# Row of `c` in the weights' queue, modulation products three loads behind and fewer at first, four places for the squares: one change in five parts to a diffusion layer on one core

## The chip, the core and the metric

The kernel runs on one core of one Trainium2 chip. The metric is the device time of one execution in microseconds (us). The engines are called PE (TensorE), DVE (VectorE), ACT (ScalarE), POOL (GpSimd) and SP (SyncE, which here only issues transfers). Each works through its own instructions in order and waits at semaphores for the others.

## What is computed

One layer for 1024 tokens of width 1024, with 256 context tokens. The parts of the reference that matter here:

```python
mod = jax.nn.silu(c) @ w_mod[l] + b_mod[l]                  # 6 x 1024 values from one row
mod_c = jax.nn.silu(c_ctx) @ w_mod[l, :, :2 * D_MODEL] + b_mod[l, :2 * D_MODEL]
h = x * (1.0 + scale1) + shift1
proj = h @ w_in + b_in                                      # q_a, k_a, v_a, q_b, k_b, v_b, gates
q_b = _rope_2d(_qk_rms(heads(OFF_QB, OFF_KB, B_HEADS), q_norm_g), rope)

def _qk_rms(t, g):
    tf = t.astype(jnp.float32)
    return (tf * lax.rsqrt(jnp.mean(tf * tf, axis=-1, keepdims=True) + QK_EPS) * g).astype(t.dtype)
```

Then follow windowed attention (A), global attention (B), their gated merge, a LayerNorm and a gated feed-forward part with a convolution. The change doesn't touch these.

## The kernel before

**Numbers in two parts.** Each matrix is split into a high part (a rounded copy, made by ACT, names `wh...`, `hh...`) and a low part (the rest, names `wl...`, `hl...`, made by DVE, for the gates by POOL). Each product takes three matmuls of 128x512: high by high, high by low, low by high (L90 to L92 in `mm3`). `split` (L82 to L87) makes the parts.

**Modulation.** The 48 columns of the modulation are no matmuls but *products* on DVE: `mod` (L188) multiplies a 128x1024 tile of weights (512 KB, by a DMA of SP) by the row `sc` (Silu of `c`, spread over the partitions by `spread`) or `scc` (the same of `c_ctx`) and sums along it. A second small instruction reads the sum out. The first 16 columns are needed for `h` and are made in the first stage, two per k. The other 48 products (16 of them with `scc` for the context, in `modx`; 32 in `modc`) are *late*: tiles `wml...`, numbered downwards from 47.

**First stage, `q1acc`.** It makes the queries of B. `load1(k)` issues, on SP's queue, two weight tiles of the modulation (`wm`), the weights `wr` and the tile `xr` of x; `modulate(k)` splits the weights, makes two products and from them `hh` and `hl` (ACT L217, L218; DVE L219). For each of eight k, 24 matmuls go into eight accumulators `q1acc0` to `q1acc7`. The row of `c` is loaded through ACT's queue (L179).

**After it.** `q_evac` moves the accumulators to `Q` with a bias (DVE L301). The PE then works through an order of gates (`g`, a column block of the gates, 48 matmuls) and products with further weights: three gates, then `qa` (queries of A, eight k of four token tiles, accumulators `accqa`), four gates, `qb` (the same for the other four token tiles, `accqb`), four gates, then `ka`, a gate, `kb` and four gates. `prefetch` loads and splits the weights of what comes later; `wg` and `wqa` share three places.

**Beside this,** the queries of B are finished in steps that `side_step` hands out. `rms_scale` makes the squares of a tile (ACT L282, into `sqq`), sums them over a head (DVE L285), divides by 64 and adds eps (DVE L286) and raises to the power -0.5 (POOL L287); then the signs are turned (POOL L322). `rope` turns a tile (L263, twice L269, L271), on POOL for tiles 2 and 5, else on DVE, with tables `tbq` that POOL makes (L274, L279). There is one tile `sqq` with places for two token tiles, so that the squares of the next wait for the sums of the one before.

**Late products.** After every gate half and every k, `mods(us)` adds that piece's matmuls to a running sum `span[0]`, and issues as many late products, load and multiplication together, as belong to its share of the whole (`span[1]`, which ends with `ka`). The places of these tiles are shared with the gates' results `sg`.

The program's order in each engine is made by a scheduler out of these pieces, so that the order in the code is not always the order on the chip.

Of the kernel before, what the change touches and what calls it, by code (L numbers as in the profile page):

```python
# [9 lines left out]
AF = mybir.ActivationFunctionType  # L10
ALU = mybir.AluOpType
# [51 lines left out]
VOFF = 0.0  # L63
VSPAN = 1.0
VSC = 0, 1
DNS = {u0 + 2 * n + (u0 == 20): (n, j0, j1) for u0, j0, j1 in ((16, 0, 4), (20, 4, 8), (24, 8, 11)) for n in range(3)}


@with_exitstack
def layer_kernel(  # L70
# [66 lines left out]
    def hput(*names):  # L137
        for n in names:
            hfree.append(hslot.pop(n))
# [21 lines left out]
    def wsplit(wr, nm, le="vector"):  # L161
        wh = ph1.tile([P, 512], R32, tag="wp", name=f"wh{nm}", bufs=8)
        wl = ph1.tile([P, 512], R32, tag="wp", name=f"wl{nm}", bufs=8)
        split(wr, wh, wl, nc.scalar, getattr(nc, le))
        return wh, wl
# [10 lines left out]
    def spread(dst, src, n):  # L176
        row = ht(f"row{n}")
        hput(f"row{n}")
        nc.scalar.dma_start(row, src.partition_broadcast(P))  # L179
        nc.scalar.activation(dst, row, AF.Silu)  # L180

    def tmp(name):
# [4 lines left out]
    def mod(w, row, bias, o):  # L187
        nc.vector.tensor_tensor_reduce(out=w, in0=w, in1=row, scale=1.0, scalar=bias, op0=ALU.mult, op1=ALU.add,  # L188
                                       accum_out=o)
# [5 lines left out]
    def load1(k):  # L195
        wm = []
        for j in (0, 1):
            w = tmp(f"wm{j}_{k}")
            nc.sync.dma_start(w, wmodT[j * 8 + k])
            wm.append(w)  # L200
        x = tmp(f"xr{k}")
        wr = raw(f"wr{k}")
        nc.sync.dma_start(wr, w_qb[k])
        nc.sync.dma_start(x, xT[k])
        st1[k] = wm, x, wr

    def modulate(k):
        wm, x, wr = st1.pop(k)
        w = wsplit(wr, f"qb{k}")
        for j in (0, 1):  # L210
            col = j * 8 + k
            mod(wm[j], sc, bmc[:, col:col + 1], modc[:, col:col + 1])
        hh = hTp.tile([P, T], R32, tag="hT", name=f"hh{k}", bufs=16)
        hl = hTp.tile([P, T], R32, tag="hT", name=f"hl{k}", bufs=16)
        a, b = modc[:, k:k + 1], modc[:, 8 + k:9 + k]
        for s in [slice(0, HALF), slice(HALF, T)] if k == 0 else [slice(0, T)]:
            nc.scalar.activation(hh[:, s], x[:, s], AF.Identity, bias=a, scale=b)  # L217
            nc.scalar.activation(x[:, s], x[:, s], AF.Identity, bias=a, scale=b)  # L218
            nc.vector.tensor_tensor(out=hl[:, s], in0=x[:, s], in1=hh[:, s].bitcast(F32), op=ALU.subtract)  # L219
        hT.append((hh, hl))  # L220
        return w
# [57 lines left out]
            eng.tensor_tensor(out=dv[:, :, a, :], in0=sv[:, :, a, :], in1=gv[:, :, 1 - a, :], op=ALU.mult)  # L279

    def rms_scale(x3, H, nm, sq, ss=None):
        nc.scalar.activation(sq.rearrange("p (h d) -> p h d", d=HD), x3, AF.Square)  # L282
        if ss is None:
            ss = ph1.tile([P, 8], F32, tag="ss", name=f"ss{nm}", bufs=4)[:, 0:H]
        nc.vector.tensor_reduce(out=ss, in_=sq.rearrange("p (h d) -> p h d", d=HD), axis=AX.X, op=ALU.add)  # L285
        nc.vector.tensor_scalar(out=ss, in0=ss, scalar1=1.0 / HD, scalar2=QK_EPS, op0=ALU.mult, op1=ALU.add)  # L286
        nc.gpsimd.tensor_tensor(out=ss, in0=ss, in1=mhalf[:, 0:H], op=ALU.pow)  # L287
        return ss

# [16 lines left out]
    def qpost(br, t):  # L306
        q = qtile(br, t)
        q3 = q.rearrange("p (h d) -> p h d", d=HD)
        if br == 0:
            def r0():  # L310
                rope(nc.gpsimd if t % 3 == 2 else nc.vector, q, q, 8, ropec[:, t], ropes[:, t], f"q0_{t}")
            return [r0]
        st = {}

        def s1():
            st["tb"] = ph1.tile([P, 2, HD], F32, tag="tb", name=f"tbq{t}", bufs=4)
            gfold(st["tb"], 0, t, nc.gpsimd)
            rms_scale(q3, 8, f"q{t}", sqq[0][:, t % 2], pqs[:, t])
            if t == NT - 1:
                sqq.clear()  # L320
                hput("sqq")
            nc.gpsimd.tensor_scalar(out=nqs[:, t], in0=pqs[:, t], scalar1=-1.0, scalar2=0.0, op0=ALU.mult, op1=ALU.add)  # L322

        def s2():
            tb = st["tb"]
            rope(nc.gpsimd if t % 3 == 2 else nc.vector, q, q, 8, tb[:, 0], tb[:, 1], f"q1_{t}")
        return [s1] + [lambda: None] * GAP + [s2]

    sqq = [ht("sqq", (P, 2, 512))]
    bias_qb = bias_tile(b_qb, "bias_qb")  # L330
    for t in range(NT):
        q_evac(1, t, acc[t], bias_qb)
# [308 lines left out]
    total = len(late)  # L641
    span = [0.0, 0.0]

    def mods(us):
        span[0] += us
        n = total - len(late)
        for _ in range(min(int(total * span[0] / span[1] + 0.01) - n, len(late))):
            col, row, o = late.pop(0)
            w = tmp(f"wml{len(late)}")
            nc.sync.dma_start(w, wmodT[col])  # L650
            mod(w, row, bmc[:, col:col + 1], o)
            if not late:
                hput("sc", "scc")
                kv_alloc()

# [1059 lines left out]
```

## Time and profile before

| what | us |
|---|---|
| three runs | 1610.99, 1612.0, 1614.45 |
| median | 1612.0 |
| the profiled execution | 1612.16 |
| its span in the trace | 1610.4 |
| granted clock of PE, mean over the span | 0.988 |
| first matmul begins | 12.94 |
| eight evacuations of `q1acc` (L301) | 54.23 to 59.68 |
| mean of a late product beside other work, 59.6 to 101.2 | 1.422 |

The prediction shows the rows of the profile. In lists of waits a row names the engine and line that waited, what it waited for, and then the sum in us, the times, and the longest wait. In the chain a row is start, length, engine, tile and line. In the timeline a row is start, length, engine, line, operation, out<-in, with the idle time ahead of it and its cause in brackets. In groups, after the bar, stand the busy time in us and the mean in ns of one instruction. Line numbers are those of the kernel before; in the change they are 2 higher from L66 on (the product L188 is L190, a split's L87 is L89) and 6 higher in the functions of the queries (L285 is L291, L286 is L292, L287 is L293, L269 is L275, L271 is L277).

### The profile page before, as it was taken

Reading aid. Unit: us, or ns where it says so; the run is one execution under the profiler, and the core shown is the slowest. Engines: PE = TensorE matmul, PEld = TensorE weight load, DVE = VectorE, ACT = ScalarE, POOL = GpSimd, SP = SyncE. Lnnn points to the kernel's source line nnn. Section 1 sums busy time; section 2 is a strip of 40 time slices with the busy share of each in tenths; the row PEclk is TensorE's granted clock in tenths of the full one; section 3 lists DMA queues with packets and bytes.
Section 4 is the critical chain, followed back from the end, with each engine's and each line's share of the span. In section 5 each row is a group of like instructions: output and inputs, shape, how many; then the busy total and the mean of one; then the engine's idle time right before and its main releaser. Section 6 shows DMA issues by size and latency. Waiting matters only on the chain.

```text
span 1610.4 us, 22060 instructions
## 1 busy us (share of the span) xinstructions
PE 1536.3 (95%) x7680; PEld 1275.4 (79%) x7680; DVE 1197.2 (74%) x1766; ACT 814.6 (51%) x1443; POOL 745.3 (46%) x731
## 2 busy tenths in 40 slices
PE   6999999999999999999999989899999999999996
PEld 5878788888877787777788877688888888888886
DVE  7797646538888777888675787588888888657886
ACT  5422222458887667688322464344544444435542
POOL 0573302526666556655323464366667765021141
PEclk9999999999999999999999999999999999999998
DMA  9695662322237555430560212233334446996821
GB/s 377 214 311 190 214 211 82 121 76 64 62 108 171 126 135 132 114 79 19 174 196 7 87 65 105 92 106 105 105 105 105 106 117 175 370 272 204 260 99 53
DMA packets 112367, 229.98 MB, mean 143 GB/s; under 512 B 12960, under 2 KB 27808, under 8 KB 112160
## 3 DMA queue, kind: packets, MB, share of 16 engines
q1 hardware_dynamic: 96816, 198.93, 37.0%
q0 software_dynamic: 10400, 20.19, 8.1%
q10 hardware_dynamic: 5040, 9.46, 1.6%
q8 instruction: 60, 0.98, 0.3%
q14 instruction: 51, 0.42, 0.1%
HBM read 177.35 MB, written 65.86 MB: 151 GB/s over the span
## 4 chain that ended last, share of the span: by engine, by line
PE 73%; DVE 10%; ACT 4%; issue 4%; DMA 4%; POOL 3%; SPq 0%; ACTq 0%; DVEq 0%; POOLq 0%
PE ptr L531 4%; PE p L92 4%; PE p L91 4%; PE p L90 4%; PE b L92 3%; PE b L91 3%; PE b L90 3%; PE g L90 2%; PE g L91 2%; PE g L92 2%; PE c L90 2%; PE c L92 2%; PE c L91 2%; PE d L90 2%; PE d L92 2%
## 5 line engine op out<-in xcount | busy, mean ns | idle before, releaser
L541 DVE TENSOR_TENSOR ptl<-ptr,pth 128x512 fp32r<-128x512 f32 x188 | 124.8, 686 | 27.7 <-ACT pth L540 25.4
L531 PE MATMUL ptr<-ident,p 128*128 128x128 f32 x816 | 126.8, 278 | 9.4 <-DVE ptl L541 6.9
L540 ACT CAST pth<-ptr 128x512 fp32r<-128x512 f32 x188 | 106.6, 588 | 56.4 <-PE ptr L531 32.8
L87 DVE TENSOR_TENSOR ld<-rd,hd 128x1024 fp32r<-128x1024 f32 x77 | 94.1, 1241 | 52.6 <-ACT hd L82 50.4
L426 ACT ACTIVATE p<-p,nm 128x1024 f32<-128x1024 f32 (+2 forms) x128 | 125.5, 982 | 11.1 <-DVE p L459 10.4
L531 PEld LDWEIGHTS ptr<-ident,p 128*128 128x128 f32 x816 | 93.7, 140 | 39.9 <-DVE ptl L541 14.0
L82 ACT CAST hd<-rd 128x1024 fp32r<-128x1024 f32 x77 | 79.4, 1053 | 81.2 <-PE p L92 51.3
L552 PE MATMUL av<-pth,VT 128*128 128x512 f32 x236 | 104.6, 443 | 1.1 <-ACT avs L558 0.5
L90 PE MATMUL p<-hd 128*128 128x512 f32 x264 | 103.2, 391 | 0.0
L92 PE MATMUL p<-hd,ld 128*128 128x512 f32 x264 | 102.7, 389 | 0.0
L91 PE MATMUL p<-ld,hd 128*128 128x512 f32 x264 | 102.7, 389 | 0.0
L90 PE MATMUL g<-hh,whg 128*128 128x512 f32 x256 | 99.9, 390 | 0.0
L92 PE MATMUL g<-hh,wlg 128*128 128x512 f32 x256 | 99.7, 389 | 0.0
L91 PE MATMUL g<-hl,whg 128*128 128x512 f32 x256 | 99.6, 389 | 0.0
L553 PE MATMUL av<-ptl,VT 128*128 128x512 f32 x236 | 97.7, 414 | 2.0 <-POOL ptl L87 1.9
L87 POOL TENSOR_TENSOR wlg<-wg,whg 128x512 fp32r<-128x512 f32 x32 | 44.4, 1393 | 111.8 <-ACT whg L82 111.8
L459 DVE TENSOR_SCALAR_CACHE_REDUCE p<-s,cvt,nmc 128x1024 f32<-128x1024 f32 x64 | 84.5, 1340 | 12.3 <-PE s L415 11.8
L414 PE MATMUL s<-KL,q 128*128 128x512 f32 (+2 forms) x192 | 76.0, 396 | 2.9 <-ACT p_x L426 2.0
L188 DVE CUSTOM_DVE_ANT_0 wml<-wml,sc,bmc 128x1024 f32<-128x1024 f32 x32 | 44.0, 1387 | 39.3 <-DMA wml<-in_wmodT_dram 38.8
L84 POOL TENSOR_SCALAR pth<-prw 128x512 fp32r<-128x512 f32 x48 | 31.2, 650 | 87.8 <-ACT prw L537 62.2
L82 ACT CAST wA<-ru 128x512 fp32r<-128x512 f32 x57 | 35.6, 625 | 71.4 <-PE d L92 33.7
L415 PE MATMUL s<-KL,q 128*128 128x512 f32 (+2 forms) x192 | 71.7, 373 | 0.0
(396 smaller groups left out, 4997.2 us busy)
## 6 DMA issues: line engine op xcount, KB each, us to landing
wml<-in_wmodT_dram SPq DMA_DIRECT2D x48, 512.0 KB
ru<-in_w_up_dram SPq DMA_DIRECT2D x38, 512.0 KB
rd<-td SPq DMA_DIRECT2D x55, 256.0 KB
rd<-sd SPq DMA_DIRECT2D x44, 256.0 KB
rd<-in_w_dn_dram SPq DMA_DIRECT2D x33, 256.0 KB
wm<-in_wmodT_dram SPq DMA_DIRECT2D x16, 512.0 KB
wg<-in_w_g_dram SPq DMA_DIRECT2D x32, 256.0 KB
sgd<-sg ACTq DMA_DIRECT2D x32, 256.0 KB
```

The costliest lines, as they stand in the source:

```text
L82: nc.scalar.copy(hi, src)
L87: lo_eng.tensor_tensor(out=lo, in0=src, in1=hi.bitcast(F32), op=ALU.subtract)
L90: nc.tensor.matmul(ps, a[0], b[0], start=start, stop=False, skip_group_check=resumed)
L91: nc.tensor.matmul(ps, a[0], b[1], start=False, stop=False, skip_group_check=resumed)
L92: nc.tensor.matmul(ps, a[1], b[0], start=False, stop=stop, skip_group_check=resumed)
L426: nc.scalar.activation(p, s, AF.Exp, bias=nm[:, h:h + 1], scale=scale, accum_out=sm[:, h:h + 1])
L459: nc.vector.tensor_scalar(out=p, in0=o, scalar1=self.qscale(nqs)[:, hs] if self.br else -1.0, scalar2=self.other[:, hs], op0=ALU.mult, op1 ...
L531: nc.tensor.transpose(tr[:, h * P:(h + 1) * P], self.pslice(h, n), ident)
L540: nc.scalar.copy(hi, tr)
L541: nc.vector.tensor_tensor(out=lo, in0=tr, in1=hi.bitcast(F32), op=ALU.subtract)
L552: nc.tensor.matmul(self.av, v, hi, start=first, stop=False)
L553: nc.tensor.matmul(self.av, v, lo, start=False, stop=self.left == 0)
```

## The change

Five parts:

1. `spread` loads the rows through SP's queue instead of ACT's: the row of `c` becomes SP's first transfer; that of `c_ctx` comes behind the loads of k = 4.
2. For k = 0, x is loaded in two halves, and the split of the weights stands behind the two products.
3. In `rms_scale`, the division by 64 moves into the Square's scale, and the addition of eps moves from DVE to POOL (18 instructions).
4. Two tiles `sqq0`, `sqq1` with two places each, instead of one.
5. `mods` issues the late loads by the share to the power 1.4 (`MODP`), so fewer early and more late, and each product is issued three loads behind its load (`MODL`), the rest at the end.

```diff
+MODP = 1.4
+MODL = 3
...
     def spread(dst, src, n):
         row = ht(f"row{n}")
         hput(f"row{n}")
-        nc.scalar.dma_start(row, src.partition_broadcast(P))
+        nc.sync.dma_start(row, src.partition_broadcast(P))
         nc.scalar.activation(dst, row, AF.Silu)
...
         nc.sync.dma_start(wr, w_qb[k])
-        nc.sync.dma_start(x, xT[k])
+        for s in [slice(0, HALF), slice(HALF, T)] if k == 0 else [slice(0, T)]:
+            nc.sync.dma_start(x[:, s], xT[k][:, s])
...
         wm, x, wr = st1.pop(k)
-        w = wsplit(wr, f"qb{k}")
+        if k:
+            w = wsplit(wr, f"qb{k}")
         for j in (0, 1):
             col = j * 8 + k
             mod(wm[j], sc, bmc[:, col:col + 1], modc[:, col:col + 1])
+        if not k:
+            w = wsplit(wr, f"qb{k}")
...
-        nc.scalar.activation(sq.rearrange("p (h d) -> p h d", d=HD), x3, AF.Square)
+        nc.scalar.activation(sq.rearrange("p (h d) -> p h d", d=HD), x3, AF.Square, scale=HD ** -0.5)
...
-        nc.vector.tensor_scalar(out=ss, in0=ss, scalar1=1.0 / HD, scalar2=QK_EPS, op0=ALU.mult, op1=ALU.add)
+        nc.gpsimd.tensor_scalar(out=ss, in0=ss, scalar1=1.0, scalar2=QK_EPS, op0=ALU.mult, op1=ALU.add)
...
-            rms_scale(q3, 8, f"q{t}", sqq[0][:, t % 2], pqs[:, t])
+            rms_scale(q3, 8, f"q{t}", sqq[t // 2 % 2][:, t % 2], pqs[:, t])
...
-    sqq = [ht("sqq", (P, 2, 512))]
+    sqq = [ht(f"sqq{n}", (P, 2, 512)) for n in (0, 1)]
...
+    wmq = []
+
     def mods(us):
         span[0] += us
         n = total - len(late)
-        for _ in range(min(int(total * span[0] / span[1] + 0.01) - n, len(late))):
+        for _ in range(min(int(total * min(span[0] / span[1], 1.0) ** MODP + 0.01) - n, len(late))):
             col, row, o = late.pop(0)
             w = tmp(f"wml{len(late)}")
             nc.sync.dma_start(w, wmodT[col])
-            mod(w, row, bmc[:, col:col + 1], o)
-            if not late:
+            wmq.append((w, row, bmc[:, col:col + 1], o))
+        while len(wmq) > (MODL if late else 0):
+            mod(*wmq.pop(0))
+            if not late and not wmq:
                 hput("sc", "scc")
                 kv_alloc()
```

The scheduler puts much else in another order with it. Three places matter for what follows. First PE, at the last k of the first stage, where an accumulator's last matmul is the one with `hl7`. Before:

```order
L90 MATMUL q1acc0_173<-whqb7_448,hh7_454 128x512
L91 MATMUL q1acc0_173<-wlqb7_449,hh7_454 128x512
L92 MATMUL q1acc0_173<-whqb7_448,hl7_455 128x512
L90 MATMUL q1acc1_174<-whqb7_448,hh7_454 128x512
L91 MATMUL q1acc1_174<-wlqb7_449,hh7_454 128x512
L92 MATMUL q1acc1_174<-whqb7_448,hl7_455 128x512
```

In the change, the same place from the ninth of its 24 matmuls on:

```order
L92 MATMUL q1acc4_178<-whqb7_449,hh7_455 128x512
L93 MATMUL q1acc4_178<-wlqb7_450,hh7_455 128x512
L92 MATMUL q1acc5_179<-whqb7_449,hh7_455 128x512
L94 MATMUL q1acc0_174<-whqb7_449,hl7_456 128x512
L94 MATMUL q1acc1_175<-whqb7_449,hl7_456 128x512
L94 MATMUL q1acc2_176<-whqb7_449,hl7_456 128x512
```

The matmuls with `hl7` moved behind the others of five tiles: `q1acc0` is complete at the 12th matmul of the 24 instead of the 3rd, `q1acc1` at the 13th instead of the 6th.

Second DVE, around the low part of the weights of `qa` for k = 2 (`wlqa2`). Before:

```order
L263 TENSOR_TENSOR rt1q1_4_975<-Q1_4_531,tbq4_930 128x512
L269 TENSOR_TENSOR rt2q1_4_976<-Q1_4_531,tbq4_930 128x16x16 x2
L285 TENSOR_REDUCE cvt_70<-sqq_522 128x8
L271 TENSOR_TENSOR Q1_4_531<-rt1q1_4_975,rt2q1_4_976 128x512
L286 TENSOR_SCALAR cvt_70<-cvt_70 128x8
L188 ISA wml33_1078,modx_63<-wml33_1078,scc_144,bmc_61 128x1024
L188 ISA modx_63 128x1
L87 TENSOR_TENSOR wlqa2_824<-wqa2_821,whqa2_823 128x512
```

In the change:

```order
L269 TENSOR_TENSOR rt1q1_6_1154<-Q1_6_536,tbq6_1068 128x512
L275 TENSOR_TENSOR rt2q1_6_1155<-Q1_6_536,tbq6_1068 128x16x16 x2
L291 TENSOR_REDUCE cvt_70<-sqq1_524 128x8
L277 TENSOR_TENSOR Q1_6_536<-rt1q1_6_1154,rt2q1_6_1155 128x512
L190 ISA wml38_1105,modx_63<-wml38_1105,scc_144,bmc_61 128x1024
L190 ISA modx_63 128x1
L190 ISA wml37_1148,modx_63<-wml37_1148,scc_144,bmc_61 128x1024
L190 ISA modx_63 128x1
L89 TENSOR_TENSOR wlqa2_811<-wqa2_808,whqa2_810 128x512
```

`wlqa2` stood behind the rope of tile 4 (and 13 late products in all); now it stands behind the rope of tile 6 (and 11 products). The first `rt2q1_6` waits on a semaphore for POOL's last step of the rope of tile 5.

Third POOL, from the second tile's power on (L287 before, L293 in the change). Before:

```order
L287 TENSOR_TENSOR cvt_70<-cvt_70,mhalf_73 128x8
L322 TENSOR_SCALAR cvt_70<-cvt_70 128x8
L87 TENSOR_TENSOR wlg2_0_640<-wg2_0_637,whg2_0_639 128x512
L263 TENSOR_TENSOR rt1q1_2_870<-Q1_2_528,tbq2_812 128x512
L87 TENSOR_TENSOR wlg2_1_646<-wg2_1_643,whg2_1_645 128x512
```

In the change:

```order
L89 TENSOR_TENSOR wlg1_1_565<-wg1_1_562,whg1_1_564 128x512
L292 TENSOR_SCALAR cvt_70<-cvt_70 128x8
L293 TENSOR_TENSOR cvt_70<-cvt_70,mhalf_73 128x8
L328 TENSOR_SCALAR cvt_70<-cvt_70 128x8
L269 TENSOR_TENSOR rt1q1_2_857<-Q1_2_530,tbq2_799 128x512
L275 TENSOR_TENSOR rt2q1_2_858<-Q1_2_530,tbq2_799 128x16x16 x2
```

`wlg1_1` moved from ahead of the first power to ahead of the second, each power has its addition of eps (L292) ahead of it on POOL, and the rope of tile 2 moved ahead of the splits `wlg2_0` and `wlg2_1`.

More of the change, by code (lines that the diff above doesn't have):

```diff
@@ L317, in s1 @@
             gfold(st["tb"], 0, t, nc.gpsimd)
-            rms_scale(q3, 8, f"q{t}", sqq[0][:, t % 2], pqs[:, t])
+            rms_scale(q3, 8, f"q{t}", sqq[t // 2 % 2][:, t % 2], pqs[:, t])
             if t == NT - 1:
                 sqq.clear()
-                hput("sqq")
+                hput("sqq0", "sqq1")
             nc.gpsimd.tensor_scalar(out=nqs[:, t], in0=pqs[:, t], scalar1=-1.0, scalar2=0.0, op0=ALU.mult, op1=ALU.add)
```

## The prediction

> **What bounds the kernel now.** The first part of the page gives the shares of the engines over the span.
>
> ```profile
> PE 1536.3 (95%) x7680; PEld 1275.4 (79%) x7680; DVE 1197.2 (74%) x1766; ACT 814.6 (51%) x1443; POOL 745.3 (46%) x731
> ```
>
> TensorE works for 1536.3 of the 1610.4 us, so an edit that doesn't take matmuls away can only gain where PE waits or runs at a lower clock. The change touches the projections and gates at the front. The second view is therefore what PE waited for in the first 480 us.
>
> ```profile
> PE q1acc L90 <- ACT hh L217: 12.9, 1, 12.9
> PE accqa L91 <- DVE wlqa L87: 2.4, 1, 2.4
> PE accqb L91 <- DVE wlqb L87: 2.0, 2, 1.5
> ...
> PE accqa L90 <- ACT whqa L82: 1.3, 1, 1.3
> ```
>
> Three places carry nearly all: the head (12.9 us before the first matmul), the `qa` product (1.3 + 2.4 = 3.7) and the `qb` product (2.0). The third view is the chain of waits through the head: start, length, engine.
>
> ```profile
> 1.17 6.65 DMA row<-in_c_row_dram
> 7.84 1.07 ACT sc L180
> ...
> 10.23 0.60 DVE wlqb L87
> 10.83 1.20 DVE wm L188
> 12.07 0.82 ACT hh L217
> 12.94 0.79 PE q1acc L90
> 13.73 0.43 PE q1acc L91
> ...
> 18.13 0.23 PE q1acc L90
> ```
>
> The row of `c` lands at 7.84 and everything behind it is a chain of single operations; the first matmuls take 0.43 us each, later ones 0.23. The fourth view is a table of stretches: time, PE, PEld, DVE, ACT and POOL busy, granted clock, DMA share, GB/s.
>
> ```profile
> 2.00:4.00 2.00, 0.00 (x0) 0.00 (x0) 0.00 (x0) 0.94 (x1) 0.00 (x0) 1.00 0.74 258
> 4.00:5.00 1.00, 0.00 (x0) 0.00 (x0) 0.17 (x1) 0.00 (x0) 0.00 (x0) 1.00 1.09 414
> 5.00:6.00 1.00, 0.00 (x0) 0.00 (x0) 0.00 (x0) 0.00 (x0) 0.00 (x0) 1.00 1.04 373
> 6.00:7.00 1.00, 0.00 (x0) 0.00 (x0) 0.00 (x0) 0.00 (x0) 0.00 (x0) 1.00 0.91 320
> 7.00:8.00 1.00, 0.00 (x0) 0.00 (x0) 0.00 (x0) 0.16 (x1) 0.00 (x0) 1.00 0.99 385
> 8.00:10.00 2.00, 0.00 (x0) 0.00 (x0) 1.06 (x1) 1.41 (x2) 0.00 (x0) 1.00 1.01 414
> 18.00:42.00 24.00, 24.00 (x107) 19.87 (x106) 21.32 (x30) 16.19 (x17) 0.00 (x0) 1.00 1.03 404
> 65.20:100.60 35.40, 32.34 (x142) 26.22 (x140) 30.54 (x51) 12.15 (x20) 32.49 (x32) 0.98 0.78 277
> 100.00:102.00 2.00, 0.75 (x2) 0.66 (x3) 2.00 (x2) 0.47 (x1) 2.00 (x2) 0.50 0.86 272
> 106.00:108.00 2.00, 2.00 (x9) 1.59 (x9) 2.00 (x7) 0.18 (x1) 0.66 (x2) 0.91 0.85 287
> ...
> 180.00:182.00 2.00, 2.00 (x10) 1.63 (x9) 1.85 (x4) 0.00 (x0) 0.00 (x0) 1.00 0.38 131
> ```
>
> Two things stand there. From 4 us the transfers run at about 400 GB/s, so what is first in the queues arrives first. And after the two `qa` waits the clock is 0.50 and 0.91 only in 106 to 108: PE went on at 101.25 (a row below follows it), so the clock is back after some 5.2 us of work at 0.43 us per matmul instead of 0.23, which is 12 matmuls by 0.2 = 2.4 us. The `qa` place thus costs 3.7 + 2.4 = **6.1 us**.
>
> **The head.** The row goes to the front of the queue that carries the weights. 512 KB are 0.52 MB. By the GB/s column 0.5 MB are in by 4 us, 1.0 by 5, 1.3 by 6, 1.7 by 7, 2.0 by 8 and 2.9 by 10. So the row lands at 4.0 to 5.0 (before: 7.84, with 2.0 MB moved), the two tiles of modulation weights behind it at 1.05 and 1.57 MB (5.3 and 6.8), `wr` and the first half of `x` at 2.1 MB: 8.1, up to 9.0 if an incomplete engine delays the last packet as it did with the row. Silu (1.07) ends by 6.0, the two products at 1.2 end by 8.4; the split of the weights now stands behind them (0.6 more), beside the transfer of `x`. Then `hh` takes 0.82 and the first matmul starts at 9.2 to 10.1; I take 9.7. That is 12.94 - 9.7 = **3.2 us** earlier (bounds 2.4 and 3.7; 0 if the row comes no sooner). Behind it PE doesn't run dry: one k of this stage needs 3.5 transfers of 0.52 MB = 1.84 MB, 4.5 us at 404 GB/s, against 24 matmuls by 24.00/107 us = 5.4. The half-clock start of the matmuls stays; it only begins sooner. The `cc` row's Silu moves behind the fourth `xr` on ACT, which is busy 16.19 of 24 us there: nothing.
>
> **From there to `qa`.** Here the gain of the head must survive. The rows are those of DVE and POOL between 54 and 102 us, from the timeline (start, length).
>
> ```profile
> 54.23 5.45 DVE L301 TENSOR_TENSOR Q<-q1acc,bias_qb 128x512 f32<-128x512 f32 x8 [5.06 <-PE q1acc L92]
> ...
> 92.85 1.28 DVE L188 CUSTOM_DVE_ANT_0 wml<-wml,scc,bmc 128x1024 f32<-128x1024 f32 x1 [0.32 <-DMA wml<-in_wmodT_dram]
> ...
> 94.67 1.86 DVE L269 TENSOR_TENSOR rt2q<-Q,tbq 128x256 f32<-128x256 f32 x2
> 96.45 0.67 DVE L285 TENSOR_REDUCE cvt<-sqq 128x8 f32<-128x512 f32 x1
> 97.04 0.68 DVE L271 TENSOR_TENSOR Q<-rt1q,rt2q 128x512 f32<-128x512 f32 x1
> ...
> 99.45 1.74 DVE L87 TENSOR_TENSOR wlqa<-wqa,whqa 128x512 fp32r<-128x512 f32 x1
> ```
>
> ```profile
> 65.23 2.03 POOL L287 TENSOR_TENSOR cvt<-cvt,mhalf 128x8 f32<-128x8 f32 x1 [2.33 <-DVE cvt L286]
> ...
> 82.19 1.65 POOL L287 TENSOR_TENSOR cvt<-cvt,mhalf 128x8 f32<-128x8 f32 x1
> ...
> 91.42 2.60 POOL L287 TENSOR_TENSOR cvt<-cvt,mhalf 128x8 f32<-128x8 f32 x1 [1.91 <-DVE cvt L286]
> ...
> 98.38 2.27 POOL L271 TENSOR_TENSOR Q<-rt1q,rt2q 128x512 f32<-128x512 f32 x1
> ```
>
> ```profile
> L287 POOL TENSOR_TENSOR cvt<-cvt,mhalf 128x8 f32<-128x8 f32 x5 | 10.8, 2154 | 4.2 <-DVE cvt L286 4.2
> ...
> L87 POOL TENSOR_TENSOR wlg<-wg,whg 128x512 fp32r<-128x512 f32 x2 | 2.6, 1294 | 0.0
> L322 POOL TENSOR_SCALAR cvt<-cvt 128x8 f32<-128x8 f32 x5 | 2.5, 501 | 0.4
> ```
>
> Before, the weights' low part `wlqa` of k = 2 is done at 99.45 + 1.74 = 101.2, and PE goes on at 101.25. Without its waits PE would have asked for it at 101.25 - 3.7 = 97.5; with the head's gain it asks at **94.3**. When does it get it? In the new order of DVE this `wlqa` stands behind the rope of tile 6, whose second half waits until POOL has finished the rope of tile 5 (before: 98.38 + 2.27 = 100.65, and `wlqa` did not wait for it). So POOL's chain decides.
>
> *Start.* The stage ends 3.2 sooner, but its last k finishes the first accumulator at the 12th matmul instead of the 3rd, 2.0 us later, so the eight evacuations start at 54.23 - 3.2 + 2.0 = 53.0 and end at 58.5. Behind them now stands the reduction (0.67) with no products ahead (59.2), then the addition of eps on POOL; the first power starts at about 59.8, against 65.23.
>
> *Length.* POOL was busy 32.5 us from 65.2 to 100.6 and idle the rest, mostly for DVE's `L286`, which is now its own. It gains one weight split (1.3) and five additions of eps. No addition of eps on POOL is in the trace: its bounds are DVE's own 0.16 (the shortest) and the like `L322` on POOL, 0.50; I take 0.4, near the row on the same engine, 2.0 in all. DVE runs two products fewer beside it; a power beside a product took 2.60 and in a stretch where DVE waited 1.65, so I take off 0.9 each. 32.5 + 1.3 + 2.0 - 1.8 = 34.0, and tile 5's rope ends at 59.8 + 34.0 = 93.8.
>
> ```profile
> L286 DVE TENSOR_SCALAR cvt<-cvt 128x8 f32<-128x8 f32 x6 | 2.7, 454 | 0.0
> L188 DVE CUSTOM_DVE_ANT_0 wml<-wml,scc,bmc 128x1024 f32<-128x1024 f32 x14 | 19.8, 1422 | 4.9 <-DMA wml<-in_wmodT_dram 4.9
> ```
>
> *Tail on DVE.* Two halves of the rope, a reduction, an addition, two products and `wlqa`: alone 0.9 + 0.67 + 0.68 + 2 x 1.28 + 0.6 = 5.4; beside POOL's big operations 1.86 + 0.67 + 0.7 + 2 x 1.42 + 1.74 = 7.8. Beside it POOL now has only 128x8 operations, and the product at 92.85 took 1.28 inside the power of 91.42, so I take 5.4: `wlqa` at 99.2, PE on at about 99.3. Gain here, with the head's gain in it and the clock lost as before: 101.25 - 99.3 = **2.0 us**. Of 3.2 + 6.1, most is eaten by this new wait of 5.0 us. Bounds: with all five powers at 1.65 and the eps at 0.16, 32.5 + 1.3 + 0.8 - 2.5 = 32.1 less the products' part gives 90.1 and `wlqa` at 95.5; with no relief and the long tail, 59.8 + 36.3 + 7.8 = 103.9, a loss of 2.7.
>
> The Trainium skill (SBUF — State Buffer, Terms) says that VectorE and GpSimd share one pair of ports, taken exclusively for the whole instruction, the loser blocked fully. That speaks against putting 18 more operations on POOL, and `wlqa`'s 1.74 beside the rope's 2.27 fits it, but the product's 1.28 inside a power doesn't; by the rule the sum here would turn into the loss worked out as the third rival.
>
> **The squares.** ACT waited 22.4 us for the one pair of places.
>
> ```profile
> ACT sqq L282 <- DVE cvt L285: 22.4, 5, 7.1
> ```
>
> ACT is 12.15 of 35.4 us busy there, and PE felt this only through the cast `whqa` behind it (the 1.3). With four places the cast is early, but `wlqa` is late next, so it is in the sum already. ACT's work on `ctx` now stands ahead of that cast and waits for two early products; both stand ahead of the rope of tile 6 on DVE, so they are ready first. The scale in Square costs nothing: the same instruction.
>
> **`qb`.** DVE waited for the loads of the products, and `wlqb` stands behind them.
>
> ```profile
> DVE wml L188 <- DMA wml<-in_wmodT_dram: 12.5, 8, 4.2
> ```
>
> With the product three loads behind its load, the load is there. PE's two waits (0.5 and 1.5) should go: **2.0 us**, 0 if the queue's blocked loads of `wqb` decide. The exponent moves products from here towards `ka`; PE has no wait there, and one product more per four costs DVE 1.4 us at a time beside matmuls: within 0.5 either way. From attention on nothing changes.
>
> **Sum.** The profiled execution took 1612.16 (median of the runs 1612.0). 1612.16 - 2.0 - 2.0 = **1608.2**.
>
> **The rivals.** *POOL's chain is short* (the lower bound). Then PE waits 1.3 or nothing, and the clock stays: behind the wait of 1.5 in `qb`, which ended ahead of 180 us, the clock reads 1.00. 1612.16 - 3.2 - 6.1 - 2.0 = 1600.9, with the short wait 1602.2. For it: POOL idled 2.9 us in the stretch for DVE. Against it: 32.5 us of its work remain. The Trainium skill (TensorE: Matmul & The Clock Gate, Part 1) puts the fall to half clock at an idle window of about 3.4 us and the return after about as much work; the 3.7 us lost in two pieces here fit the first, the 5.2 us back are longer. Chance 0.25.
>
> *The gain is eaten whole.* `wlqa` comes at 101 as before, or the head gives nothing because the row shares its engines with the same loads anyway (`wlqa` 3.2 later, at 102.4): 1612.16 + 0 to 1.2, less 2.0 or 0: 1610.2 to 1612.2. Chance 0.22.
>
> *DVE blocked by each small POOL operation.* Three powers beside the tail, 1.65 to 2.15 each, would put 5 to 6.5 us on it: `wlqa` at 105, 1612.16 + 3.7 - 2.0 = 1613.9. Chance 0.06.
>
> *Slower: POOL late at tile 5.* From 95.8 on (101.2 less 5.4) the rope of tile 5 makes `wlqa` later than before. If POOL still idles 2.9 us, for the reductions, and nothing relieves it, it ends at 59.8 + 36.3 + 2.9 = 99.0; with the tail of 7.8 `wlqa` comes at 106.8, 5.6 late: 1615.8, and 1617.8 if `qb` keeps its waits. Against it: the reductions wait for fewer products than before. Chance 0.09.
>
> **How the numbers follow.** My forecast has 0.38, and by itself reaches from 1606 to 1610.5. A time within 0.2% (3.2 us) can't be told from no change here; faster means below 1608.8. That holds for the first rival (0.25) and about 0.30 of the forecast's 0.38: 0.55. Slower (over 1615.2) is the last rival: 0.09. The rest is 0.36. The range takes in the first rival and the bounds of the unknown costs, and leaves out the last rival: 1600.9 to 1614.9, the upper end being the upper bound (a loss of 2.7) with `qb` unchanged.
>
> **What would show it.** First matmul at 9.2 to 10.1 rather than 12.94, the row landed by 5. The first power at about 60 and tile 5's rope done at 94: if at 91, the first rival; at 99, the last. One wait of PE for `wlqa` of about 5 us with half clock for 5 us behind it; none for `whqa`; none for `wlqb`. A DVE product stretched beyond 2 us beside a power speaks for the blocked ports. I am wrong if PE waits at a place that it didn't before, above all for `wlg` (whose splits now stand behind ropes on POOL) or in `ka`.

## The result and the profile after

| | before | after |
|---|---|---|
| median of five runs, us | 1612.88 | 1622.73 |
| lowest to highest | 1610.99 to 1614.45 | 1620.72 to 1624.74 |
| ratio, 95% interval | | 1.0065 [1.0052, 1.0077] |
| the profiled execution, its span | 1612.16, 1610.4 | 1624.59, 1622.8 |

The change makes the kernel slower by 0.65%, outside the forecast's range. The first part of the profile's page after, then the longest of PE's waits at the front:

```profile
PE 1541.6 (95%) x7680; PEld 1278.3 (79%) x7680; DVE 1184.7 (73%) x1748; ACT 813.0 (50%) x1443; POOL 742.8 (46%) x749
```

```profile
PE q1acc L92 <- ACT hh L223: 10.6, 1, 10.6
PE accqb L93 <- DVE wlqb L89: 8.8, 4, 6.5
PE accqa L92 <- ACT whqa L84: 3.2, 1, 3.2
PE accqa L93 <- DVE wlqa L89: 3.1, 1, 3.1
```

Nothing is new in kind: the same three places carry nearly all. The head fell from 12.9 to 10.6, `qa` rose from 3.7 to 6.3, and `qb` from 2.0 to 8.8. Where the 12.4 us of the spans' difference arise is read by setting landmarks beside each other, the start of the first or last matmul of a group in the timeline:

| start of | before | after | difference |
|---|---|---|---|
| first matmul | 12.9 | 10.6 | -2.3 |
| last high-by-high matmul of `q1acc` | 58.1 | 56.4 | -1.7 |
| last of `accqa` | 119.2 | 121.3 | +2.1 |
| last of `accqb` | 187.1 | 198.1 | +11.0 |
| last of `accka` | 257.8 | 268.8 | +11.0 |
| first attention score | 345.1 | 355.7 | +10.6 |
| end of the span | 1610.4 | 1622.8 | +12.4 |

So 3.8 us go in `qa` and 8.9 in `qb`. From the score to the end it is 1265.3 before and 1267.1 after; in the other profiles of this study that stretch is 1262 to 1270 long, so nothing is read out of its 1.8.

**The head after.** The chain of waits (start, length, engine):

```profile
1.19 5.80 DMA wm<-in_wmodT_dram
...
7.14 1.21 DVE wm L190
...
8.44 0.59 DVE wm L190
...
9.76 0.82 ACT hh L223
...
10.63 0.80 PE q1acc L92
```

No row of `c` stands in it any more. The row landed at 5.65 by the timeline of ACT, and its Silu ended at 6.71; what DVE waits for, until 6.99, is a tile of modulation weights, a transfer issued behind the row.

**`qa` after.** DVE, POOL and ACT in the timeline:

```profile
90.14 1.67 DVE L190 CUSTOM_DVE_ANT_0 wml<-wml,scc,bmc 128x1024 f32<-128x1024 f32 x1 [4.24 <-DMA wml<-in_wmodT_dram]
...
92.93 2.31 DVE L190 CUSTOM_DVE_ANT_0 wml<-wml,scc,bmc 128x1024 f32<-128x1024 f32 x1
...
96.44 1.28 DVE L190 CUSTOM_DVE_ANT_0 wml<-wml,scc,bmc 128x1024 f32<-128x1024 f32 x1
...
97.65 0.69 DVE L269 TENSOR_TENSOR rt1q<-Q,tbq 128x512 f32<-128x512 f32 x1
...
102.53 0.69 DVE L89 TENSOR_TENSOR wlqa<-wqa,whqa 128x512 fp32r<-128x512 f32 x1
```

```profile
57.07 3.80 POOL L89 TENSOR_TENSOR wlg<-wg,whg 128x512 fp32r<-128x512 f32 x3 [3.54 <-ACT whg L84]
...
61.56 1.71 POOL L293 TENSOR_TENSOR cvt<-cvt,mhalf 128x8 f32<-128x8 f32 x1
...
92.49 1.67 POOL L277 TENSOR_TENSOR Q<-rt1q,rt2q 128x512 f32<-128x512 f32 x1
```

```profile
98.21 0.60 ACT L639 ACTIVATE cx<-cx,modx 128x256 f32<-128x256 f32 x1 [10.42 <-DMA cx<-in_ctxT_dram]
...
98.73 0.62 ACT L84 CAST whqa<-wqa 128x512 fp32r<-128x512 f32 x1
```

POOL is on time: the rope of tile 5 ends at 94.16. DVE isn't: it stood 4.24 us for a late load until 90.14, and the rope of tile 6 begins at 97.65, three products later. ACT isn't either: the work on `ctx`, ahead of the cast `whqa` in its order, stood 10.42 us for its own load.

**`qb` after.** Here SP's timeline is set beside that of before. A row is the first issue's start, the time until the last of them is issued, and, behind the names, how many. First before, then after:

```profile
145.50 0.38 SPq L628 DMA_DIRECT2D wqb<-in_w_qa_dram  x1
147.83 0.33 SPq L650 DMA_DIRECT2D wml<-in_wmodT_dram  x1
151.84 2.56 SPq L628 DMA_DIRECT2D wqb<-in_w_qa_dram  x2
155.34 0.33 SPq L650 DMA_DIRECT2D wml<-in_wmodT_dram  x1
155.76 0.86 SPq L628 DMA_DIRECT2D wqb<-in_w_qa_dram  x2
```

```profile
138.91 0.38 SPq L634 DMA_DIRECT2D wqb<-in_w_qa_dram  x1
144.86 7.43 SPq L658 DMA_DIRECT2D wml<-in_wmodT_dram  x5
152.38 0.86 SPq L634 DMA_DIRECT2D wqb<-in_w_qa_dram  x2
159.51 2.60 SPq L658 DMA_DIRECT2D wml<-in_wmodT_dram  x5
166.66 0.33 SPq L634 DMA_DIRECT2D wqb<-in_w_qa_dram  x1
```

Between the weights of k = 0 and those of k = 3 stood two late loads; now there are ten. On DVE the products of these loads stand ahead of the splits:

```profile
163.43 1.28 DVE L190 CUSTOM_DVE_ANT_0 wml<-wml,sc,bmc 128x1024 f32<-128x1024 f32 x1 [2.62 <-DMA wml<-in_wmodT_dram]
164.73 1.28 DVE L190 CUSTOM_DVE_ANT_0 wml<-wml,sc,bmc 128x1024 f32<-128x1024 f32 x1
165.94 0.69 DVE L89 TENSOR_TENSOR wlqb<-wqb,whqb 128x512 fp32r<-128x512 f32 x1
...
177.22 1.28 DVE L190 CUSTOM_DVE_ANT_0 wml<-wml,sc,bmc 128x1024 f32<-128x1024 f32 x1 [3.02 <-DMA wml<-in_wmodT_dram]
178.54 1.28 DVE L190 CUSTOM_DVE_ANT_0 wml<-wml,sc,bmc 128x1024 f32<-128x1024 f32 x1
179.75 0.69 DVE L89 TENSOR_TENSOR wlqb<-wqb,whqb 128x512 fp32r<-128x512 f32 x1
```

Before, the first split of `qb` ran at 153.78, ten microseconds ahead of the first matmul of `accqb` (163.4); now it runs at 165.94, with PE there at 165.5. The last row here is the split for k = 2; before, it began at 168.93. The clock pays once more (time, PE, PEld, DVE, ACT, POOL busy, granted clock, DMA share, GB/s):

```profile
176.00:178.00 2.00, 0.00 (x0) 0.00 (x0) 0.78 (x1) 0.39 (x1) 0.00 (x0) 0.72 0.77 287
...
180.00:182.00 2.00, 1.51 (x4) 1.22 (x5) 1.64 (x3) 0.00 (x0) 0.00 (x0) 0.50 0.95 328
182.00:184.00 2.00, 2.00 (x7) 1.56 (x6) 0.66 (x1) 0.00 (x0) 0.00 (x0) 0.57 1.00 391
184.00:186.00 2.00, 1.71 (x8) 1.11 (x7) 2.00 (x4) 0.62 (x1) 0.00 (x0) 1.00 0.40 162
```

PE did 7 matmuls in 182 to 184, at clock 0.57.

### The profile page after: what moved, and what is told of

The parts are those of the page before. It is cut to its first block, busy times and chain, and to the rows that moved or that the text cites. A ratio compares the mean times of both kernels' runs of the same rounds, so it can differ in the third digit from the quotient of the medians.

```text
span 1622.8 us, 22074 instructions
## 1 busy us (share of the span) xinstructions
PE 1541.6 (95%) x7680; PEld 1278.3 (79%) x7680; DVE 1184.7 (73%) x1748; ACT 813.0 (50%) x1443; POOL 742.8 (46%) x749
## 4 chain that ended last, share of the span: by engine, by line
PE 75%; DVE 11%; POOL 4%; ACT 4%; DMA 3%; issue 3%; SPq 0%; ACTq 0%; DVEq 0%; POOLq 0%
PE ptr L537 5%; PE p L93 3%; PE p L92 3%; PE p L94 3%; PE b L94 3%; PE b L93 3%; DMA wml<-in_wmodT_dram 3%; PE b L92 3%; PE s L420 2%; PE av L558 2%; PE av L559 2%; PE c L92 2%; PE c L94 2%; PE c L93 2%; PE d L94 2%
## 5 line engine op out<-in xcount | busy, mean ns | idle before, releaser
L432 ACT ACTIVATE p<-p,nm 128x1024 f32<-128x1024 f32 (+2 forms) x128 | 125.3, 981 | 11.2 <-DVE p L465 10.4
```

Source lines behind the costliest of these rows:

```text
L432: nc.scalar.activation(p, s, AF.Exp, bias=nm[:, h:h + 1], scale=scale, accum_out=sm[:, h:h + 1])
```

## The experiments

Of all runs the table gives what the readings below need: the late loads that SP issued from 137 to 190 us, those between the weights of k = 0 and k = 3 of `qb` in its order, the start of the first split `wlqb`, PE's waits in `qa` and `qb`, and the start of the first attention score.

| run | late loads 137 to 190 | between k = 0 and 3 | first `wlqb` | waits `qa` | waits `qb` | first score | ratio [95%] |
|---|---|---|---|---|---|---|---|
| before | 12 | 2 | 153.8 | 3.7 | 2.0 | 345.1 | 1 |
| after | 21 | 10 | 165.9 | 6.3 | 8.8 | 355.7 | 1.0065 [1.0052, 1.0077] |
| e1 | 16 | 7 | 161.3 | 4.4 | 7.2 | 349.9 | 1.0049 [1.0031, 1.0067] |
| e2 | 20 | 10 | 170.7 | 11.2 | 7.4 | 360.4 | 1.0115 [1.0094, 1.0136] |
| e3 | 12 | 2 | 152.2 | 3.9 | 1.9 | 342.8 | 1.0006 [0.9993, 1.002] |
| e4 | 17 | 8 | 167.2 | 4.9 | 7.2 | 355.3 | 1.0076 [1.0056, 1.0096] |
| e5 | 16 | 7 | 163.4 | 4.3 | 8.1 | 351.9 | 1.0057 [1.0041, 1.0073] |
| e6 | 12 | 2 | 151.3 | 3.1 | 2.5 | 342.1 | 0.9994 [0.9982, 1.0006] |
| e7 | 16 | 11 | 164.5 | 5.0 | 6.9 | 351.8 | 1.0036 [1.0021, 1.0052] |
| e8 | 9 | 3 | 161.9 | 6.9 | 3.0 | 349.4 | 1.0025 [1.0007, 1.0044] |
| e9 | 16 | 7 | 170.7 | 6.9 | 8.0 | 358.5 | 1.0066 [1.0049, 1.0084] |
| e10 | 12 | 2 | 153.8 | 4.7 | 3.9 | 345.6 | 0.9998 [0.9985, 1.0012] |
| e11 | 17 | 8 | 166.2 | 6.3 | 7.8 | 354.9 | 1.0065 [1.0044, 1.0087] |
| e12 | 18 | 9 | 166.4 | 2.1 | 6.9 | 351.7 | 1.0056 [1.0042, 1.0071] |
| e13 | 21 | 10 | 158.5 | 6.0 | 4.5 | 352.4 | 1.0035 [1.002, 1.0049] |
| e14 | 19 | off SP | 166.2 | 6.4 | 11.1 | 358.8 | 1.0088 [1.0069, 1.0108] |
| e15 | 19 | off SP | 153.8 | 6.4 | 0 | 352.0 | 1.0052 [1.0034, 1.007] |
| e16 | 12 | 2 | 151.2 | 3.0 | 0 | 338.4 | 0.9974 [0.9961, 0.9987] |

### Which part of the change does it

**e1, the changed kernel without part 5** (`mods` as before). 1618.6 us.

> The change with its fifth part taken back (late products as before: linear, each beside its load); all else as changed. Theory 1, late products: in the changed kernel ACT's stores of the gates' results wait for older late loads, ACT's casts queue behind them, and the work on ctx stands ahead of a cast of qa. Both come from part 5, so PE's waits in qb fall from 8.8 us to 2 to 4 and in qa from 6.3 to about 4, and the time is 1608 to 1613 us. Rival, the other four parts (one pair more of places, eps on POOL, the order that the scheduler makes of them) cost it: 1618 us or more, with the waits in qb still above 6.

**e2, the gate results stored by POOL.** ACT issues the stores of `sg`, and in the trace after it stands there until late loads have landed (`ACT whqb` waits 19.9 us for late loads in 155 to 195). Why a store should wait for a load that it doesn't use, no run here shows. 1630.15 us.

```diff
-        nc.scalar.dma_start(sgd[f][:, s], sg)
+        nc.gpsimd.dma_start(sgd[f][:, s], sg)
```

> The change with the stores of the gates' results issued by POOL instead of ACT, so that no cast of ACT queues behind a store that waits. Theory 1: PE's waits in qb fall from 8.8 to 3 us or less and the time to 1613 to 1617 us; the waits in qa stay (the work on ctx still stands ahead of a cast). Rival, more late loads in qb than the transfers carry: the loads are late whoever issues the stores, qb stays at 7 us or more and the time at 1620 to 1624 us.

**e3, the kernel before with parts 1 and 2 alone.** 1611.34 us.

> The kernel before with the first two parts alone (row of c first in the weights' queue, x in halves and the split behind the products for k = 0). Both theories: first matmul at about 10.6 us instead of 12.94. If the wait in qa is set by the chain on POOL and DVE that starts with the first stage's end, the gain lasts: 1610.3 to 1611 us (2.3 less). If it is set by transfers and places, it is eaten there: 1612.5 to 1613 us.

**e4, the kernel before with part 5 alone** (`MODP = 1.4`, `MODL = 3`). 1622.71 us.

> The kernel before with the fifth part alone (exponent 1.4 and a lag of three loads). Theory 1: the loss is there without the other parts, PE waits 6 us or more in qb, and the time is 1618 to 1624 us. Rival, it needs the other parts with it: PE's waits in qb stay at 2 to 3 us and the time within 1611 to 1615 us.

What follows: part 5 alone costs as much as the whole change (e4), but without it the change still costs 0.5% (e1). So it is not the only cause. Freeing ACT from the stores makes it worse (e2, `qa` 11.2), so ACT's standing there is not what PE lacks. The head is worth 2.3 us at the first score (e3: 342.8 against 345.1), but in the time it can't be told from no change. Next, the second part that could do it, and the place that theory 2 names: late tiles, gate results and the second pair of squares take places in turn from one list.

**e5, the kernel before with part 4 alone** (four places for the squares). 1620.67 us.

> The kernel before with the fourth part alone (two tiles with two places each for the squares). Theory 2, places: tiles of late products share their places with the gates' results, so one more place taken for the squares changes which late load waits for which store of a gate's result; those waiting loads stand in SP's queue ahead of the weights of qb. Before has one such load between the weights of k = 0 and k = 4, this kernel three. It expects waits of PE in qb of 6 us or more (2.0 before) and 1615 to 1620 us. Rival, the squares only matter together with eps on POOL or with the earlier head: qb stays at 2 to 3 us and the time at 1610 to 1613 us or a little below, since ACT waits less for the sums.

**e6, the kernel before with parts 1 to 3.** 1609.95 us.

> The kernel before with parts 1 to 3 (head, and eps on POOL), one tile of squares and late products as before. Theory 2: SP's order around the weights of qb is the same as before, so PE waits about 2 us there; scores of the attention begin 2 to 3 us earlier than before (345.1), and the time is 1607 to 1611 us. Rival, eps on POOL makes its chain longer and costs in qa: the attention begins no earlier than before and the time is 1612 to 1616 us.

**e7, the changed kernel with two places of their own for the gate results**, so that no late tile waits for a store. 1617.69 us.

```diff
-        if late:
+        if False:
             sg = ht(f"sg{f}_{hf}", (P, HALF))
...
         else:
             sg = ph1.tile([P, HALF], F32, tag="sg", name=f"sg{f}_{hf}", bufs=2)
```

> The whole change, but the gates' results always in two places of their own, so that no late load waits for a store of a gate's result. Theory 2: the loss in qb goes, PE waits there 3 us or less (8.8 in the change), and the time falls to 1612 to 1616 us. Rival, the order on DVE (late products ahead of the low parts of qb) or the amount of transfers makes the loss: 6 us or more remain in qb and the time is 1620 us or more. ACT may wait for the two places when stores are slow, which would show as gates waiting.

**e8, the changed kernel with the late products of `qb` put into the other groups.** 1615.42 us.

```diff
-                  for gi, _ in order[:order.index((0, KT - 1)) + 1])
+                  for gi, _ in order[:order.index((0, KT - 1)) + 1] if gi not in (3,))
...
-        mods(3 * len(tiles))
+        if gi not in (3,):
+            mods(3 * len(tiles))
```

> The whole change, but no late product is issued in the eight steps of qb (their share goes to the other stages). Theory 2 and its rival on the amount of transfers both expect less waiting in qb: 3 us or less and 1613 to 1617 us. If qb still waits 6 us or more, the loads issued before it are what stands in the queue.

What follows: one line, the second pair of squares, costs 0.57% by itself (e5), with no edit anywhere near `qb`. Parts 1 to 3 cost nothing (e6). The stores' waits are not needed for the loss: with places of their own (e7) `qb` still waits 6.9, so theory 2 fell in that form. Taking late loads out of `qb` (e8: 9 of them in place of 21) brings its waits to 3.0; the time stays 0.25% above before, and `qa` waits 6.9 there. Hence theory 3: what counts is how many late loads stand among the weights of `qb`, whatever put them there.

**e9, the kernel before with the exponent alone** (`MODP = 1.4`, `MODL = 0`). 1623.21 us.

> The kernel before with the exponent 1.4 of the late products' share alone (no lag). Theory 3 (what stands between the weights of k = 0 and k = 3 of qb in SP's in-order queue decides: 8 late loads there with the exponent, 2 before, and the lag does not alter them): PE waits about 7 us in qb, the first attention score at 354 to 356, 1619 to 1623. Rival (the lag of three products does the harm of part 5): qb waits 2 to 3, the score near 345, 1610 to 1613.

**e10, e6 with the lag alone added** (`MODP = 1.0`, `MODL = 3`). 1611.25 us.

> The kernel before with parts 1 to 3 of the change and, of part 5, only the lag of three products (the share linear as before; one pair of squares). Theory 3: SP's order in qb is that of before (2 late loads between the weights of k = 0 and k = 3), so PE waits 2 to 3 us in qb, the first attention score at 340 to 343, 1606 to 1611. Rival (the lag does the harm): qb waits about 7, the score at 350 or later, 1616 to 1620. If theory 3 holds, this is also a candidate for a kernel faster than before.

**e11, the changed kernel without part 4.** 1621.32 us.

> The changed kernel without part 4 (one pair of places for the squares as before; head, eps, exponent and lag as changed). Theory 3: 8 late loads stand between the weights of k = 0 and k = 3, so qb waits about 7, the first attention score at 350 to 354 (the exponent's 355 less the head's and the eps' 3), 1616 to 1621. Rival (the two parts harm only together, through the places of the squares): qb waits 2 to 4, the score at 342 to 346, 1608 to 1613.

**e12, the kernel before with parts 1 and 2, and e8's edit.** 1620.62 us.

> The kernel before with parts 1 and 2 (head), and the late products of qb put into the other groups. Theory 3: few late loads stand ahead of the weights of qb, so PE waits 1 to 3 us there; qa stays near the 3.9 of the head alone; the first attention score at 341 to 345, 1607 to 1612. Rival (the late products cost the same wherever they stand, since all have to be loaded): the score at 347 to 350, 1613 to 1616, with new waits in ka or the gates.

What follows: of part 5 it is the exponent (e9) that fills `qb`, not the lag (e10: 12 late loads, like before). The lag isn't free, though: against e6, to which it was added, `qa` waits 1.6 us more, `qb` 1.4 more, and the first score comes 3.5 us later, past the 340 to 343 that was expected; the time can't be told from no change. Parts 4 and 5 each suffice and don't add up: e11, without part 4, loses as much as the whole change. e12 missed its total, and for a reason that helps: the edit meant to empty `qb` left 18 late loads there, more than the 12 of before (why the scheduler put them there was not followed up); its waits of 6.9 fit the 18. Over all kernels with the splits on DVE the waits in `qb` are 1.9 to 3.9 us with 9 to 12 late loads in 137 to 190, and 6.9 to 11.1 with 16 to 21. Nothing lies between. Within the upper group more loads don't mean a longer wait: 8.1 and 8.0 with 16 (e5, e9), 6.9 with 18 (e12).

### Which queue makes PE wait

In these runs both queues fill together, SP's with loads and DVE's with products. The next four part them.

**e13, the changed kernel with the splits of `qb` on POOL**, idle from 147 to 194 us after the change. 1617.66 us.

```diff
-        ready[gi, k] = wsplit(wr, f"{nm}{k}"), c
+        ready[gi, k] = wsplit(wr, f"{nm}{k}", "gpsimd" if nm == "qb" else "vector"), c
```

> The changed kernel with the low splits wlqb of the weights of qb on POOL, which does nothing from 147 to 194 us of the changed kernel; SP's order of loads stays that of the changed kernel (10 late loads between the weights of k = 0 and k = 3). Theory D (DVE's order decides: the splits stand behind products that wait for their loads): PE waits 0 to 3 us in qb instead of 8.8, the first attention score at 346 to 349 instead of 355.7, 1612 to 1616. Rival S (the weights' transfers behind the late loads on SP decide): qb waits 6 to 9, the score at 353 to 356, 1619 to 1624.

**e14, the changed kernel with the weights of `qb` loaded through POOL's queue.** 1626.46 us.

```diff
-        nc.sync.dma_start(wr, src[k])
+        (nc.gpsimd if nm == "qb" else nc.sync).dma_start(wr, src[k])
```

> The changed kernel with the transfers of the weights of qb issued by POOL instead of SP; the splits stay on DVE behind the products (28 products ahead of the split of k = 0, 7 more ahead of that of k = 2; the changed kernel has 27 and 6). Theory D: PE still waits 6 to 9 us in qb, 1619 to 1624. Rival S: qb waits 0 to 3, 1612 to 1616.

**e15, both edits.** 1619.25 us.

> The changed kernel with both: splits of qb on POOL and their weights' transfers issued by POOL. Theory D: as with the splits alone, 0 to 3 us in qb, 1612 to 1616. Rival S: as with the weights alone, the same figure. If both queues hold PE in turn, only this one comes near 1612.

**e16, e6 with the edit of e13.** 1609.34 us.

> The kernel before with parts 1 to 3 of the change, and the low splits of the weights of qb on POOL; no lag, no exponent, one pair of squares. Theory D: PE waits 0 to 1.5 us in qb instead of 2.5, the first attention score at 339 to 341, 1606 to 1610. Rival S: qb waits 2 to 3 as with parts 1 to 3 alone, 1608 to 1612.

The waits of PE in e13, then what POOL, which issues the weights, waited for in e14 (timeline), then PE's wait in e15 and SP's issues there:

```profile
PE accqb L92 <- ACT whqb L84: 3.0, 1, 3.0
...
PE accqb L93 <- POOL wlqb L89: 1.5, 2, 0.8
```

```profile
146.02 0.56 POOL L634 DMA_DIRECT2D wqb<-in_w_qa_dram  x1 [0.30 <-POOL wlg L89]
167.23 0.54 POOL L634 DMA_DIRECT2D wqb<-in_w_qa_dram  x1 [20.65 <-DVE wlqb L89]
```

```profile
PE g L92 <- ACT whg L84: 6.1, 1, 6.1
```

```profile
143.42 43.62 SPq L658 DMA_DIRECT2D wml<-in_wmodT_dram  x19
187.22 0.33 SPq L628 DMA_DIRECT2D wg<-in_w_g_dram  x1
```

e14 speaks for theory D (DVE's order decides). Its first three weights are issued by 146, out of SP's way, and PE waits longer still (11.1), because the splits stand behind products. The fourth weights then wait 20.65 us for a split to free their place, so late splits also make late loads. e13 took the splits away from there: the waits halve to 4.5, not to D's 0 to 3 (nor does the time reach its 1612 to 1616), and the longest is now for the cast of a weight. Its transfers ran at 332 and 341 GB/s in 155 to 170 and 170 to 185 us (299 and 307 in the changed kernel, 246 and 262 before). e15 frees both, and `qb` waits for nothing; yet it is no faster than e13, since the next gate's weights stand behind 19 late loads on SP, and PE waits 6.1 there. Neither theory alone named that.

So DVE's order decides where PE pays (e13, e15). That the late loads put into that stretch decide that it pays rests on e8 and on the two groups of kernels. How they do it stays open. One reading is their bytes: 9 more than before by 0.52 MB are 4.7 MB, by an estimate 11.6 us at the 404 GB/s of the prediction's rows, about the size of the 8.9 lost in `qb`. But by the same estimate the 4 more of e5 and e9 would cost 5.2 us, and `qb` waits 8.1 and 8.0 there; and the transfers of the changed kernel ran at 274 GB/s from 137 to 190 us (223 before), so by the 404 they had room. The other reading is that the two queues hold each other. From 142 to 190 us SP stood 24.1 us at late loads, until a product of DVE was done (12.1 before), and 13.9 us at weights of `qb`, until a split of DVE was done (4.2 before), while DVE stood for the loads. No run changed the bytes alone, so neither reading is shown.

e16 applies D's edit where the queues are as before: no wait in `qb`, the score at 338.4, and a time below that of both kernels, 0.9974 [0.9961, 0.9987]. The gain is small: its median lies 0.16% below before's 1611.85, and three of its twelve runs, at 1602.4 to 1604.2, stand apart from the others; the profiled one is among them. Its interval overlaps with that of e6, so what the moved splits add to parts 1 to 3 is shown for the wait and not for the total.

## Why the prediction was wrong

**The head: right in direction, too large.** 2.3 us instead of 3.2 (first matmul 10.63, predicted 9.2 to 10.1). The row came at 5.65 for a predicted 4.0 to 5.0, and the weights of the first product at 6.99 for a predicted 5.3; both were summed from 414 GB/s in 4 to 5 us, and after the change it is 254 there and 398 in 5 to 6. So the first product began at 7.14, and all behind it took the time that was put down for it.

**POOL's chain: right.** The rope of tile 5 ended at 94.16 for a predicted 93.8. It began late (61.56 for 59.8, behind three splits for the gates until 60.87) and was shorter (32.6 for 34.0). Eight additions of eps took a mean of 490 ns (predicted 400).

**DVE's tail: the length right, the start wrong.** From 97.65 to `wlqa` done at 103.22 are 5.6 us for a predicted 5.4. But the prediction let it begin when POOL was done; DVE was by then behind three products, and those behind a load for which it had stood 4.24 us.

**"ACT's work on `ctx` ... waits for two early products ... they are ready first": wrong.** It waited for its own load, which no term priced and which SP issued only at 93.42, behind six late loads from 83.08 on; the cast behind it cost PE 3.2. With this, `qa` lost 3.8 us where 1.2 of the head's 3.2 had been expected to go. Which part does this isn't settled. A wait for this cast of 2.5 us or more stands only in kernels with parts 4 and 5 together (the change, e2, e13 to e15), though not in all of them (e7, e8); without one of the two, PE's waits in `qa` sum to 2.1 to 6.9 us.

**The step that failed: the `qb` term.** "With the product three loads behind its load, the load is there. PE's two waits (0.5 and 1.5) should go: 2.0 us." They became 8.8, and with the clock 8.9 us of path. Two sentences carried it. The lag was to let the products find their loads landed; DVE's wait for late loads up to 340 us is 58.8 us after the change; with the lag on e6 it is 46.6 (e10), without it 43.5 (e6). In `qb` the lag changed nothing in the order: in the timelines of e10 and e6 late loads and weights on SP, and products and splits on DVE, come in the same order. And "the exponent moves products from here towards `ka`", priced "within 0.5 either way", is reversed: with the exponent alone, late loads from 137 to 190 rise from 12 to 16, and those behind 190 fall from 10 to 9 (e9). What it takes from the front lands in `qb` and just ahead of it (from 100 to 137 us, 12 in place of 9). The squares were priced only at ACT, where they did what was said (wait for the sums down from 22.4 to 6.2 us), not by what they do to `qb`: alone they raise its late loads from 12 to 16 (e5). That they do it through the places of the late tiles is the likely way, but was not followed up.

**The rivals.** None fits: the one on the slower side put the loss on POOL at tile 5, and POOL was on time. (The second rival's own upper end was added up wrongly: 1612.16 + 1.2 is 1613.4, not 1612.2. Nor does the lower bound of the head's gain, 2.4, follow from its latest start: 12.94 - 10.1 is 2.8.) That "DVE is blocked by small POOL operations" fell:

```profile
95.23 1.28 DVE L190 CUSTOM_DVE_ANT_0 wml<-wml,scc,bmc 128x1024 f32<-128x1024 f32 x1
```

```profile
95.38 2.65 POOL L293 TENSOR_TENSOR cvt<-cvt,mhalf 128x8 f32<-128x8 f32 x1
```

This product, begun 0.15 us ahead of a power of POOL, took its 1.28 us, and so did the next (96.44), which lies wholly inside the power; the one at 92.93 took 2.31 beside the rope's 128x512 piece. The power took 2.65 there and 1.64 at its shortest, so whether POOL is the one held up isn't settled. The Trainium skill (SBUF — State Buffer, Terms) has VectorE and GpSimd lock each other out of a shared port pair for a whole instruction; the trace is in line with that for the large operation, and for DVE beside the power it isn't.

**The sum.** Head and `qa` were to give 2.0 at the end of `qa` and gave -2.1; `qb` was to give 2.0 and gave -8.9. These two make 15.0 of the 16.4 us between 1608.2 and the profiled 1624.59. "I am wrong if PE waits at a place that it didn't before" was the wrong test: it waits where it did before, only longer.

## What to carry to other kernels

Before an edit to a share, a place or a lag is priced at the spot it names, count in the scheduled order of each in-order queue what stands ahead of the instructions that a waiting engine needs, before and after: ten late loads among the weights in place of two gave this loss away, and no duration did. Work that is put off doesn't vanish, so look at the stretch that receives it, for transfers as for engines. An operation that PE waits for shouldn't stand in one engine's order with work that waits for loads if another engine idles there: moving eight splits to POOL took away PE's waits there (2.5 us in e6, none in e16), and that version, with parts 1 to 3, is the only one faster than before, by 0.3%.

## What the runs showed that was not expected

Parts that look unrelated don't add up: part 4 costs 0.57%, part 5 0.76%, and together with parts 1 to 3 they cost 0.65%. Each puts late loads into the same stretch (16 and 17 there in place of 12, 21 together), and the wait of PE there doesn't grow with them. And the clock: four waits of PE in `qa` of at most 1.5 us, 3.1 in sum, left it at 1.00 (e6), while a single wait of 3.9 halved it (e3). The stretch of 100 to 102 us of e6, then of e3:

```profile
100.00:102.00 2.00, 2.00 (x10) 1.61 (x10) 2.00 (x3) 0.52 (x1) 1.92 (x2) 1.00 1.01 358
```

```profile
100.00:102.00 2.00, 2.00 (x6) 1.52 (x6) 2.00 (x4) 0.12 (x1) 1.13 (x3) 0.50 0.85 254
```

The Trainium skill (TensorE: Matmul & The Clock Gate, Part 1) gives an idle window of about 3.4 us for the fall; these two agree with it. For the return it gives about as much work. In `qb` that agrees: PE goes on at 180.49, and the last half-clock stretch is 182 to 184, at 0.57. In `qa` it doesn't: PE goes on at 103.27, and the matmuls in the timeline shorten from 0.63 to 0.39 us only from 108.56 on, 5.3 us later.
